# Background steps, store queues and early loads in a one-core step of a hybrid encoder with expert lookup

## The chip, the core and the metric

The kernel runs on one core of a Trainium2 chip. The metric is device microseconds of one execution, the median of several runs. The engines named here are TensorE (PE; its weight loads are PEld), VectorE (DVE), ScalarE (ACT), GpSimd (POOL) and SyncE (SP), which in this kernel only starts transfers. Each engine takes its instructions in order. A transfer that an engine starts sits in that engine's instruction stream, and if it has to wait for something, all that stands behind it on that engine waits too.

## What is computed

One layer of a streaming encoder on 512 prompt tokens and 8 x 16 sample tokens, all in float32:

```python
z = rmsnorm(x, norm_mix_g) @ w_in              # q, k, v, u, vs, gate a, gate b
o = attend(q, k, v, bias, mask, sinks)          # sliding window, a table of relative positions as bias
s = sgu(gelu(u), rmsnorm(gelu(vs)), w_s, b_s)   # chunked spatial gating
x = x + (sigmoid(ga) * (o @ w_pa) + sigmoid(gb) * (s @ w_pb)) @ w_out
xn = rmsnorm(x, norm_ffn_g)
q = xn @ w_query                                # 8 heads, two halves, 128 keys each
# top 16 of the 16 x 16 sums of the two halves' top 16 -> 16 experts per head, g = softmax
y = x + sum over the 128 chosen experts e of g_e * gelu(U[e] . xn) * V[e]
y = rmsnorm(y, norm_final_g)
```

The outputs are y and the new key, value and gating rows. There are 16384 experts with rows of 2048 numbers in U and in V.

## The kernel before

The tokens form five tiles of 128: four prompt tiles (0 to 3) and the sample tile (4, `SAMPLE`). They go in two groups: G1 = (0, 4) first, then G2 = (1, 2, 3). Every projection is a call of `gemm`, which walks over the weight rows in steps of 256: a 512 KB load (`raw`, four buffers) by SP, and for each 128 rows a rounding copy `whi` by ScalarE (L143) and the rest `wlo` by VectorE (L144). TensorE multiplies three times for each tile: x-high with `whi`, x-high with `wlo`, x-low with `whi` (L211 to L213).

The experts are treated in two ways. The tiles of G1 gather: `gather_peer` reads the 128 chosen rows of U, then those of V, one row for each token at a time, 1 MB per gather (L754, by GpSimd), with a product on VectorE for each (L740, L745), and closes with `finish` (norm, scaling L726, store of y L727). The tiles of G2 go dense: `dense_peer` multiplies with all of U in 32 blocks of 512 experts (`U(s)`), weighs the result with a matrix of gates (`wd`, built in `weights` for every token by a matmul of two one-hot products, L789 to L799), and multiplies with all of V in 16 blocks of 1024 experts, each in four column blocks (`V(b, nb)`).

Two queues of generators fill the gaps. `side` holds small work (attention, gating, routing, `weights`, the late steps); `pump`, called after every 256 rows, takes steps from it at a rate of `steps[0]`. `bg` holds the two `gather_peer` generators, tile 0 and then the sample tile; `tick` takes from it at half the GEMM's rate per 256 rows, and these instructions get a low priority. A scheduler orders the instructions of each engine from these priorities, so an order on an engine need not be the order in the code.

The places that the change and the prediction speak of:

- Start. `prep` loads the x tiles transposed (`xT`), scales them and splits them; `start_rows` takes its steps inside the first GEMM (keys and values, `w_kv`) and puts the rest at the front of `side` in its last but one step. `bias_table` looks up the bias rows by a matmul and stores them, repeated 32 times, to `bvd` in device memory (768 KB from 16 partitions). `sample_consts` loads what the sample tile's attention needs: the cached keys and values (`kcT`, `vc`), its new values after a trip through device memory (`vnd`, `vn`), the sinks and the bias.
- Dense stage, first part: U blocks 0 to 11 (`LEAD`) run ahead of any V block. Their activations are stored to device memory (`ad`, L831), since the gates are not ready yet; `late` reads them back. After block 11 the work pools are closed and opened anew with other sizes.
- Dense stage, second part: V blocks 0 to 15, and from block 5 on the U blocks 12 to 31 between them. `RATE_C` is the rate of the background steps in V blocks 0 to 4, `RATE_D` in all later U and V blocks, and `RATE_T` in the last six V column blocks, from where on gathers take their buffers from a larger pool (`deep`, tiles named `m`).
- End: the last V blocks' sums get their squares (L850) and the factor `gfin` (L853), then the row norms scale 12 pieces of 128 x 512, by ScalarE every third (L890) and VectorE the others (L892), and each is stored (L893).

Of the kernel before, what the change touches and what calls it, by code (L numbers as in the profile page):

```python
# [27 lines left out]
RATE_Q = 0.6  # L28
RATE_W = 1.2
RATE_C = 1.3  # L30
RATE_D = 1.63
SQ = 0.6
SW = 1.6
SA = 0.8
# [25 lines left out]
def body(tc, A, O):  # L60
    nc = tc.nc
    with ExitStack() as ctx:
# [22 lines left out]
        def mtile(shape, dt=F32):  # L85
            return mt.tile(shape, dt, name=nm("m"), tag="m")
# [135 lines left out]
        def bias_table():  # L222
            tab = evs((32, 16))
            nc.sync.dma_start(tab, A["table"])
            oh = evs((32, 384))
            nc.sync.dma_start(oh, A["onehot"])
            p = misc()
            nc.tensor.matmul(p[:16, :384], tab, oh, start=True, stop=True)
            bv = evs((16, 384))
            nc.vector.tensor_copy(bv, p[:16, :384])  # L230
            nc.sync.dma_start(bvd, bv.unsqueeze(1).to_broadcast([16, 32, 384]))
            for _ in range(5):
                yield


# [76 lines left out]
        def sample_consts(vnat, out):  # L312
            vnd = dr.tile([128, 128], F32, name="vnd")
            nc.sync.dma_start(vnd, vnat)
            yield
            kc = mtile([128, 2, 8, 128])
            nc.vector.memset(kc, 0.0)
            for kv in range(2):
                nc.sync.dma_start(kc[kv * 64:kv * 64 + 64, kv], A["kcT"][kv * 64:kv * 64 + 64])
            vc = mtile([128, 8, 128])  # L320
            nc.sync.dma_start(vc, A["vc"])
            sk = stat(2)
            nc.sync.dma_start(sk, A["sinks_s"])
            bias = slot((128, 2, 144))
            for kv in range(2):
                nc.sync.dma_start(bias[:, kv, :],
                                  bass.AP(tensor=bvd.tensor, offset=bvd.offset + kv * 8 * 32 * 384 + 127,
                                          ap=[[32 * 384, 8], [383, 16], [1, 144]]))
            vn = mtile([16, 8, 128])
            nc.sync.dma_start(vn, vnd.rearrange("(b t) d -> t b d", b=8))  # L330
            out.extend((kc, vc, vn, sk, bias))
            yield

# [441 lines left out]
        def weights(ti, ijg):  # L775
# [7 lines left out]
            for t0 in range(0, 128, 4):  # L783
# [12 lines left out]
                    nc.tensor.matmul(pw[:, t - t0, :], a, b, start=True, stop=True)  # L796
                w = slot((128, 4, 128))
                nc.scalar.copy(w, pw)  # L798
                nc.sync.dma_start(wd[ti][t0:t0 + 4, :].rearrange("t (i j) -> i t j", i=128), w)  # L799
                yield  # L800

        def dense_peer(G, x2T, r2, x1d):
            n = len(G)
            ad = [[dr.tile([128, 512], F32, name=nm("ad")) for _ in G] for _ in range(LEAD)]
            if True:
# [20 lines left out]
                def U(s, ticks):  # L826
                    def ev(i, ps):
                        a = abuf()
                        nc.scalar.activation(a, ps, AF.Gelu_apprx_tanh, scale=r2[i])
                        if s < LEAD:  # L830
                            nc.sync.dma_start(ad[s][i], a)  # L831
                        else:
                            side.append(h_step(s, i, a))
                    gemm(x2T, 0, KC, A["UT"][s], ev, ticks)
# [50 lines left out]
                for c in range(4):  # L885
                    cs = slice(c * 512, c * 512 + 512)
                    for i, ti in enumerate(G):
                        t = y[i, c]
                        if (c * n + i) % 3 == 0:
                            nc.scalar.activation(t, t, AF.Copy, scale=r[i])  # L890
                        else:
                            nc.vector.tensor_scalar_mul(t, t, r[i])  # L892
                        nc.sync.dma_start(O["y"][ti][:, cs], t)  # L893

        G1, G2 = (0, SAMPLE), (1, 2, 3)
        x1a, r1a, x1b, r1b = [], [], [], []
        start = prep(G1, x1a, r1a, [(i, c) for c in range(4) for i in range(2)])
        next(start)
        next(start)
        side.append(bias_table())  # L900

        def start_rows(kc):
            if kc % 2 == 0 and kc:
                next(start)
                next(start)
            if kc == 6:
                side.insert(0, start)

        nextg = prep(G2, x1b, r1b, [(i, c) for i in range(3) for c in range(4)])

# [103 lines left out]
```

## Time and profile before

| what | us |
|---|---|
| median of 3 runs (lowest, highest) | 3988.98 (3987.25, 3996.61) |
| the profiled execution | 3996.57 |
| its span, first to last instruction | 3994.9 |
| first matmul starts | 7.43 |
| last matmul starts | 3976.26 |
| TensorE busy | 3883.8 |
| VectorE busy | 3153.5 |
| ScalarE busy | 1728.2 |
| GpSimd busy | 829.1 |

The profiled execution is 7.6 us above the median; 1.7 us of it lie outside the span. Busy times are sums over the span; what an engine was idle for, and what ended the wait, is read from the timeline and from the waits. The windows give the same sums for a stretch.

### The profile page before, as it was taken

How to read it: one execution, taken by the hardware profiler on the slowest of the kernel's cores; microseconds unless marked ns; L12 is line 12 of the kernel's file. 1: busy time of each engine (PE TensorE's matmuls, PEld its weight loads, DVE VectorE, ACT ScalarE, POOL GpSimd, SP SyncE). 2: the span in 40 equal slices, each digit the busy share in tenths (PEclk: the TensorE clock that was granted, in tenths of full speed). 3: DMA queues.
4: the chain of work that ended last, by engine and by line, in shares of the span. 5: the costliest groups of instructions: out<-in, count | busy, mean ns of one | idle time of the engine just before them, and what ended most of it. 6: DMA issues, size and time to landing. Idle time of an engine off the chain costs nothing. (4 is left out here: it accounts for less than half of the span.)

```text
span 3994.9 us, 52665 instructions
## 1 busy us (share of the span) xinstructions
PE 3883.8 (97%) x17880; PEld 3177.5 (80%) x17880; DVE 3153.5 (79%) x5421; ACT 1728.2 (43%) x3338; POOL 829.1 (21%) x678
## 2 busy tenths in 40 slices
PE   8999998999999999999999899999999999999998
PEld 6778786877777888877878788877888888888886
DVE  4655769966767987899977688878888888888888
ACT  5665554444444334436665333333333333333333
POOL 1000113211212223211111112222222222222222
PEclk9999999999999999999999999999999999999999
DMA  7666786777878997569988989989998999999987
GB/s 224 204 187 208 248 264 201 273 276 279 311 277 286 336 334 249 206 198 314 327 264 288 338 325 338 342 299 365 338 350 336 353 331 345 345 340 349 346 337 290
DMA packets 333919, 1180.51 MB, mean 296 GB/s; under 512 B 35840, under 2 KB 94784, under 8 KB 267088
## 3 DMA queue, kind: packets, MB, share of 16 engines
q1 hardware_dynamic: 259824, 640.15, 47.9%
q0 software_dynamic: 73824, 536.99, 35.0%
q8 instruction: 141, 2.31, 0.2%
q14 instruction: 130, 1.06, 0.1%
HBM read 1117.69 MB, written 59.31 MB: 295 GB/s over the span
## 5 line engine op out<-in xcount | busy, mean ns | idle before, releaser
L211 PE MATMUL acc<-whi,m 128*128 128x512 f32 (+1 forms) x5232 | 2066.7, 395 | 23.3 <-ACT whi L143 18.3
L212 PE MATMUL acc<-wlo,m 128*128 128x512 f32 (+1 forms) x5232 | 2049.8, 392 | 22.5 <-DVE wlo L144 22.4
L213 PE MATMUL acc<-whi,m 128*128 128x512 f32 (+1 forms) x5232 | 2044.1, 391 | 0.3 <-DVE m L144 0.2
L143 ACT CAST whi<-raw 128x512 fp32r<-128x512 f32 (+1 forms) x1888 | 1157.9, 617 | 1979.3 <-PE acc L213 1646.6
L144 DVE TENSOR_TENSOR wlo<-raw,whi 128x512 fp32r<-128x512 f32 (+1 forms) x1824 | 1221.5, 689 | 526.8 <-ACT whi L143 523.1
L212 PEld LDWEIGHTS acc<-wlo,m 128*128 128x128 f32 x5232 | 990.7, 189 | 227.1 <-DVE wlo L144 34.5
L211 PEld LDWEIGHTS acc<-whi,m 128*128 128x128 f32 x5232 | 989.3, 189 | 225.4 <-ACT whi L143 20.6
L213 PEld LDWEIGHTS acc<-whi,m 128*128 128x128 f32 x5232 | 989.5, 189 | 202.7 <-DVE m L144 0.8
L740 DVE SCALAR_TENSOR_TENSOR gb<-gb,xa 128x2048 f32<-128x2048 f32 x256 | 589.6, 2303 | 79.5 <-DMA gb<-in_U,idx 69.1
L745 DVE SCALAR_TENSOR_TENSOR xa<-gb,hw,xa 128x2048 f32<-128x2048 f32 x239 | 560.3, 2344 | 70.4 <-DMA gb<-in_V,idx 64.1
L754 POOL DMA_INDIRECT gb<-in_V,idx x239 | 318.5, 1333 | 1228.8 <-DVE wlo L144 331.2
L754 POOL DMA_INDIRECT gb<-in_U,idx x256 | 339.6, 1327 | 1018.9 <-ACT whi L143 366.2
L144 POOL TENSOR_TENSOR wlo<-raw,whi 128x512 fp32r<-128x512 f32 x64 | 91.5, 1431 | 261.8 <-ACT whi L143 229.7
L796 PEld LDWEIGHTS pm<-s 128*128 128x128 f32 x768 | 102.6, 193 | 30.5 <-ACT s L793 14.6
L796 PE MATMUL pm<-s 128*128 128x128 f32 x768 | 113.7, 283 | 10.0 <-DVE s L789 8.0
L789 DVE TENSOR_SCALAR s<-io,S 128x128 f32<-128x128 f32 x384 | 114.8, 339 | 3.6 <-DMA wd<-s 3.6
L847 DVE TENSOR_TENSOR s<-s,acc 128x512 f32<-128x512 f32 x180 | 112.5, 678 | 0.0
L144 DVE TENSOR_TENSOR m<-pm,m 128x512 fp32r<-128x512 f32 (+1 forms) x142 | 93.5, 661 | 7.5 <-ACT m L143 6.5
L143 ACT CAST m<-pm 128x512 fp32r<-128x512 f32 (+1 forms) x142 | 79.6, 563 | 16.3 <-PE pm L362 6.3
L798 ACT COPY s<-pm 128x512 f32<-128x512 f32 x96 | 56.5, 588 | 64.8 <-PE pm L796 64.2
L814 DVE TENSOR_TENSOR b<-b,b 128x512 f32<-128x512 f32 x36 | 24.8, 688 | 56.0 <-DMA b<-wd 53.5
L792 ACT ACTIVATE s<-io,S 128x128 f32<-128x128 f32 x192 | 66.7, 398 | 3.6 <-DVE S L782 2.3
(194 smaller groups left out, 1668.7 us busy)
## 6 DMA issues: line engine op xcount, KB each, us to landing
raw<-in_UT SPq DMA_DIRECT2D x256, 512.0 KB, 6.2
raw<-in_VP SPq DMA_DIRECT2D x256, 512.0 KB, 6.5
raw<-in_w_in SPq DMA_DIRECT2D x224, 512.0 KB, 4.6
raw<-in_w_out SPq DMA_DIRECT2D x64, 512.0 KB, 5.4
raw<-in_w_q SPq DMA_DIRECT2D x64, 512.0 KB, 4.5
wd<-s SPq DMA_DIRECT2D x96, 256.0 KB, 6.0
b<-wd SPq DMA_DIRECT2D x96, 256.0 KB, 5.2
raw<-in_w_pa SPq DMA_DIRECT2D x32, 512.0 KB, 4.2
```

The source lines that it names most:

```text
L143: mark[0] = nc.scalar.copy(hi, src).ins
L144: (E or nc.vector).tensor_sub(lo, src, hi.bitcast(F32))
L211: nc.tensor.matmul(o, xh, hi, start=(k == 0), stop=False)
L212: nc.tensor.matmul(o, xh, lo, start=False, stop=False)
L213: nc.tensor.matmul(o, xl, hi, start=False, stop=(k == K - 1))
L740: q = nc.vector.scalar_tensor_tensor(t, t, 1.0, xg, op0=ALU.mult, op1=ALU.mult, accum_out=dots[:, j:j + 1])
L745: q = nc.vector.scalar_tensor_tensor(y, t, hw[:, j:j + 1], y, op0=ALU.mult, op1=ALU.add)
L754: d = nc.gpsimd.indirect_dma_start(out=t, out_offset=None, in_=src, in_offset=bass.IndirectOffsetOnAxis(ap=idx[j // 32][:, j % 32:j % 32 + ...
L789: nc.vector.tensor_scalar(a, io128, tr[:, 0, t:t + 1], tr[:, 2, t:t + 1], op0=ALU.is_equal, op1=ALU.mult)
L792: nc.scalar.activation(b, io128, AF.Abs, bias=tr[:, 3, t:t + 1])
L796: nc.tensor.matmul(pw[:, t - t0, :], a, b, start=True, stop=True)
L847: nc.vector.tensor_add(y[i, nb], x1, ps)
```

## The change

Four groups of edits. `RATE_D` rises from 1.63 to 1.72. The `wd` and `ad` stores are started by ScalarE instead of SP, and so is every third of the last stores of y, the one that ScalarE has scaled itself. `bias_table` is no longer in `side` from the start: it is appended behind `start` near the end of the first GEMM, and it gives up three steps behind its work instead of five. In `sample_consts` the loads of `vn` and the sinks come first, the `kcT`, `vc` and bias loads are divided by two more `yield`s, and the memset of the key tile moves from VectorE to GpSimd.

```diff
@@ -28,7 +28,7 @@
 RATE_Q = 0.6
 RATE_W = 1.2
 RATE_C = 1.3
-RATE_D = 1.63
+RATE_D = 1.72
 SQ = 0.6
 SW = 1.6
 SA = 0.8
@@ -229,7 +229,7 @@
             bv = evs((16, 384))
             nc.vector.tensor_copy(bv, p[:16, :384])
             nc.sync.dma_start(bvd, bv.unsqueeze(1).to_broadcast([16, 32, 384]))
-            for _ in range(5):
+            for _ in range(3):
                 yield
 
 
@@ -313,21 +313,23 @@
             vnd = dr.tile([128, 128], F32, name="vnd")
             nc.sync.dma_start(vnd, vnat)
             yield
+            vn = mtile([16, 8, 128])
+            nc.sync.dma_start(vn, vnd.rearrange("(b t) d -> t b d", b=8))
+            sk = stat(2)
+            nc.sync.dma_start(sk, A["sinks_s"])
             kc = mtile([128, 2, 8, 128])
-            nc.vector.memset(kc, 0.0)
+            nc.gpsimd.memset(kc, 0.0)
             for kv in range(2):
                 nc.sync.dma_start(kc[kv * 64:kv * 64 + 64, kv], A["kcT"][kv * 64:kv * 64 + 64])
+                yield
             vc = mtile([128, 8, 128])
             nc.sync.dma_start(vc, A["vc"])
-            sk = stat(2)
-            nc.sync.dma_start(sk, A["sinks_s"])
+            yield
             bias = slot((128, 2, 144))
             for kv in range(2):
                 nc.sync.dma_start(bias[:, kv, :],
                                   bass.AP(tensor=bvd.tensor, offset=bvd.offset + kv * 8 * 32 * 384 + 127,
                                           ap=[[32 * 384, 8], [383, 16], [1, 144]]))
-            vn = mtile([16, 8, 128])
-            nc.sync.dma_start(vn, vnd.rearrange("(b t) d -> t b d", b=8))
             out.extend((kc, vc, vn, sk, bias))
             yield
 
@@ -796,7 +798,7 @@
                     nc.tensor.matmul(pw[:, t - t0, :], a, b, start=True, stop=True)
                 w = slot((128, 4, 128))
                 nc.scalar.copy(w, pw)
-                nc.sync.dma_start(wd[ti][t0:t0 + 4, :].rearrange("t (i j) -> i t j", i=128), w)
+                nc.scalar.dma_start(wd[ti][t0:t0 + 4, :].rearrange("t (i j) -> i t j", i=128), w)
                 yield
 
         def dense_peer(G, x2T, r2, x1d):
@@ -828,7 +830,7 @@
                         a = abuf()
                         nc.scalar.activation(a, ps, AF.Gelu_apprx_tanh, scale=r2[i])
                         if s < LEAD:
-                            nc.sync.dma_start(ad[s][i], a)
+                            nc.scalar.dma_start(ad[s][i], a)
                         else:
                             side.append(h_step(s, i, a))
                     gemm(x2T, 0, KC, A["UT"][s], ev, ticks)
@@ -890,21 +892,20 @@
                             nc.scalar.activation(t, t, AF.Copy, scale=r[i])
                         else:
                             nc.vector.tensor_scalar_mul(t, t, r[i])
-                        nc.sync.dma_start(O["y"][ti][:, cs], t)
+                        (nc.scalar if (c * n + i) % 3 == 0 else nc.sync).dma_start(O["y"][ti][:, cs], t)
 
         G1, G2 = (0, SAMPLE), (1, 2, 3)
         x1a, r1a, x1b, r1b = [], [], [], []
         start = prep(G1, x1a, r1a, [(i, c) for c in range(4) for i in range(2)])
         next(start)
         next(start)
-        side.append(bias_table())
 
         def start_rows(kc):
             if kc % 2 == 0 and kc:
                 next(start)
                 next(start)
             if kc == 6:
-                side.insert(0, start)
+                side.extend([start, bias_table()])
 
         nextg = prep(G2, x1b, r1b, [(i, c) for i in range(3) for c in range(4)])
```

## Rows read from the trace of the kernel before

**Rows 1.** Part 1 of the page: busy time of each engine, its share of the span and its instructions.

```profile
PE 3883.8 (97%) x17880; PEld 3177.5 (80%) x17880; DVE 3153.5 (79%) x5421; ACT 1728.2 (43%) x3338; POOL 829.1 (21%) x678
```

**Rows 2.** Windows, late dense part: stretch in us and its length; then busy us and instructions of TensorE, its weight loads, VectorE, ScalarE and GpSimd; granted TensorE clock, mean busy share of the DMA engines, GB/s.

```profile
2750.00:3300.00 550.00, 550.00 (x2476) 455.03 (x2475) 466.79 (x584) 191.68 (x314) 144.80 (x108) 1.00 0.92 344
```

**Rows 3.** Windows of the start, columns as in rows 2.

```profile
12.00:16.00 4.00, 4.00 (x23) 4.00 (x22) 2.67 (x6) 1.68 (x5) 0.00 (x0) 1.00 0.86 96
...
16.00:20.00 4.00, 2.05 (x18) 1.84 (x16) 2.33 (x3) 0.34 (x1) 0.00 (x0) 1.00 0.91 102
...
24.00:28.00 4.00, 4.00 (x19) 4.00 (x20) 2.25 (x6) 1.95 (x6) 1.43 (x2) 0.50 1.02 316
```

**Rows 4.** Timeline of the SP queue at the start: start us, duration us, engine, line, operation, out<-in, count (x2 with a long duration spans the time between the two).

```profile
10.88 0.70 SPq L231 DMA_DIRECT2D bvd<-e  x1
...
11.62 4.74 SPq L426 DMA_DIRECT2D S<-in_xT  x2
...
19.95 0.90 SPq L426 DMA_DIRECT2D S<-in_xT  x2
...
41.77 1.18 SPq L319 DMA_DIRECT2D m<-in_kcT  x2
...
43.00 0.58 SPq L321 DMA_DIRECT2D m<-in_vc  x1
...
46.04 11.33 SPq L198 DMA_DIRECT2D raw<-in_w_in  x7
```

**Rows 5.** Timeline of TensorE at the start, two instructions before which it was idle; in brackets the idle us and what ended them.

```profile
23.07 0.58 PE L211 MATMUL acc<-whi,m 128*128 128x256 f32 x1 [5.02 <-ACT m L143]
...
52.40 0.49 PE L211 MATMUL acc<-whi,m 128*128 128x512 f32 x1 [3.59 <-ACT whi L143]
```

**Rows 6.** Timeline of GpSimd at the start: the first operation after its loads of `xT` tiles.

```profile
64.50 0.20 POOL L282 MEMSET S<- 64x128 f32 x1 [35.81 <-DMA S<-bvd]
```

**Rows 7.** Timeline of the SP queue at the border of the U and V blocks.

```profile
2184.76 0.33 SPq L198 DMA_DIRECT2D raw<-in_UT  x1
...
2205.38 1.68 SPq L831 DMA_DIRECT2D ad<-S  x3
...
2207.22 0.34 SPq L198 DMA_DIRECT2D raw<-in_VP  x1
```

**Rows 8.** Timeline at the same border: TensorE's last transposes of old tiles, ScalarE's activation of the last U block, TensorE's first matmul of the V block.

```profile
2193.11 0.60 PE L818 MATMUL pm<-ident,b 128*128 128x128 f32 x4
...
2204.66 2.05 ACT L829 ACTIVATE S<-acc,stats 128x512 f32<-128x512 f32 x3 [8.22 <-PE acc L213]
...
2212.34 0.80 PE L211 MATMUL acc<-whi,m 128*128 128x512 f32 x1 [6.37 <-ACT whi L143]
```

**Rows 9.** The `wd` stores (L799) and `ad` stores (L831) by source line: count, shortest, median and longest issue in ns, first and last start.

```profile
L799 SPq DMA_DIRECT2D wd<-s x96: 359/360/1568, 1809.1 to 2158.8; - x96
...
L831 SPq DMA_DIRECT2D ad<-S x36: 319/332/1321, 1715.0 to 2206.7; - x36
```

**Rows 10.** Window of the stretch with the `wd` stores, columns as in rows 2.

```profile
1809.00:2165.00 356.00, 346.04 (x1859) 289.23 (x1858) 308.92 (x739) 233.12 (x621) 51.03 (x42) 0.99 0.91 302
```

**Rows 11.** The SP queue's own waits, whole span: who waited for what, us in total, times, longest.

```profile
SPq L799 <- ACT s L792: 150.4, 82, 5.1
```

**Rows 12.** Timeline near 2050 us, VectorE and TensorE.

```profile
2049.20 0.69 DVE L814 TENSOR_TENSOR b<-b,b 128x512 f32<-128x512 f32 x1 [8.68 <-DMA b<-wd]
...
2050.89 2.04 PE L796 MATMUL pm<-s 128*128 128x128 f32 x8 [8.03 <-DVE s L789]
```

**Rows 13.** Line 754 by source: the gathers into the deep buffers (`m` tiles): count, shortest, median and longest ns, first and last start.

```profile
L754 POOL DMA_INDIRECT m<-in_V,idx x17: 936/2149/3593, 3876.5 to 3957.2; - x17
```

**Rows 14.** Timeline of VectorE in the tail.

```profile
3967.05 4.73 DVE L745 SCALAR_TENSOR_TENSOR xa<-m,hw,xa 128x2048 f32<-128x2048 f32 x2
...
3977.32 0.68 DVE L853 TENSOR_TENSOR s<-s,b 128x512 f32<-128x512 f32 x1
...
3978.40 2.35 DVE L726 SCALAR_TENSOR_TENSOR xa<-xa,stats,m 128x2048 f32<-128x2048 f32 x1 [0.39 <-DMA m<-in_gfin]
...
3980.67 1.29 DVE L853 TENSOR_TENSOR s<-s,b 128x512 f32<-128x512 f32 x2
...
3982.76 0.49 DVE L892 TENSOR_SCALAR s<-s,stats 128x512 f32<-128x512 f32 x1
```

**Rows 15.** Timeline of the SP queue in the tail.

```profile
3980.78 0.34 SPq L727 DMA_DIRECT2D out_y<-xa  x1
...
3983.36 7.28 SPq L893 DMA_DIRECT2D out_y<-s  x12
```

**Rows 16.** Windows of the tail, columns as in rows 2.

```profile
3985.00:3988.00 3.00, 0.00 (x0) 0.00 (x0) 1.08 (x3) 0.17 (x1) 0.00 (x0) 0.50 1.04 378
...
3990.00:3992.00 2.00, 0.00 (x0) 0.00 (x0) 0.00 (x0) 0.00 (x0) 0.00 (x0) 0.50 1.04 384
...
3992.00:3994.00 2.00, 0.00 (x0) 0.00 (x0) 0.00 (x0) 0.00 (x0) 0.00 (x0) 0.50 0.27 99
```

**Rows 17.** The first finish (tile 0): VectorE's wait, SP's `y` store, and the window of 2660 to 2670 us.

```profile
2662.81 2.35 DVE L726 SCALAR_TENSOR_TENSOR xa<-xa,stats,gb 128x2048 f32<-128x2048 f32 x1 [6.81 <-DMA gb<-in_gfin]
...
2665.19 0.34 SPq L727 DMA_DIRECT2D out_y<-xa  x1
...
2660.00:2670.00 10.00, 10.00 (x46) 8.01 (x45) 7.19 (x10) 6.01 (x9) 1.25 (x1) 1.00 0.69 248
```

## The prediction

> **What bounds the kernel now.** I read the page's busy shares first: TensorE is busy 97% of the span [rows 1]. That is an average, so the next view is the windows of the late dense part: there TensorE is busy all the time, 550.00 of 550 us, with VectorE at 467 us and the DMA engines at a share of 0.92 [rows 2]. Nothing that only unloads another engine can shorten that part. A gain has to come from places where TensorE stands still, so I looked for these in the timeline: the first 55 us, the border between the dense stage's first twelve U blocks and its V blocks (near 2205 us), one hole near 2050 us, and the tail after the last matmul near 3976 us. The diff touches each of the four.
>
> **Start: the bias table is emitted later.** Before, `bias_table` runs in the first GEMM. Its store to `bvd` goes to the SP queue at 10.88 us; the two `xT` loads behind it take SP 4.74 us instead of the 0.9 us of such a pair, and the last pair goes out at 19.95 us [rows 4]. From 12 to 20 us the DMA engines are 0.86 to 0.91 busy and yet move 96 to 102 GB/s [rows 3]: 8 us at about 99 GB/s is 0.79 MB, which is that one store (16 x 32 x 384 x 4 bytes = 0.79 MB). TensorE waits 5.02 us at 23.07 us for the `xT` chunk that was behind it [rows 5], and from 24 to 28 us it runs at a granted clock of 0.50, which costs another 2 us [rows 3]. The change emits the table after the remaining `start` steps, so the store leaves this place: minus 5.0 us, with up to 2 us of clock on top. The store still has to run. Pump steps are counted alike (2 left of `start`, 1+5 of the table and 2 of `sample_consts` become 2, 1+3 and 4), so attention starts at the same step, and the store now falls into the first Q block, some 38 to 50 us. There TensorE has a second hole, 3.59 us at 52.40 us [rows 5]: `kcT` and `vc`, 1 MB in all, went out before the next weight load, at 46.04 us [rows 4]. Spread over three steps they no longer do; the 8 us of the store come instead. I set these two against each other. The bounds: 0 (the whole hole comes back at the new place) to 5.0+2.0+3.6 = 10.6 us gained. I take 5. The `kc` memset goes from VectorE to GpSimd, which stands idle 35.81 us there [rows 6]; at 0.20 us for 128 columns of half the partitions, 2048 columns are at most 16 x 0.20 = 3.2 us, hidden in that idle time; without it, `sample_consts` would be that much later.
>
> **Border of U and V: activation stores by ScalarE.** SP issues one raw load at 2184.76 us and then stands at the first `ad` store until 2205.38 us, since the store waits for ScalarE's gelu of the last U block; the first load for V, queued behind it, goes out at 2207.22 us [rows 7]. TensorE is then idle 6.37 us until 2212.34 us [rows 8]. On ScalarE's queue the same store waits where its producer is, and SP is free. The V loads reuse the space of the old tiles, whose last reader among the `b` tiles is the transpose at 2193.11 us [rows 8], so a load could be out some 13 us earlier than 2207.22 us, enough for the hole to vanish. Against this, the order in which ScalarE takes the new casts and the gelu is not known: if the gelu stays first, its three pieces end near 2206.7 us [rows 8] and only a cast and a subtraction are left, a hole of some 2 us. So minus 2 to minus 6.4 us if SP is freed, 0 if the loads don't move; I take minus 4.
>
> **Gate stores by ScalarE.** 96 `wd` stores cost SP 0.36 us each and 36 `ad` stores 0.33 us (longest 1.57 and 1.32 us) [rows 9]. ScalarE has issued no DMA in this run, so its price is bounded by nothing below and 1.57 us above; I take SP's, 96 x 0.36 = 35 us between 1809 and 2165 us, where ScalarE has 356 - 233 = 123 us idle [rows 10]. That idle time hides them; without it each issue delays the next cast by its own length. VectorE is 309 of 356 us busy there and waits for those casts, so some leaks out: plus 1 us (0 to 8). SP stops waiting for these copies, 150.4 us in 82 waits [rows 11], but TensorE loses only 10 us in this stretch [rows 10], and 8.03 of them are one chain, VectorE waiting 8.68 us for a load of gates just stored [rows 12]. An earlier store could shorten it: 0 to minus 8, taken as 0.
>
> **More background steps.** Each loop step of a GEMM adds half the rate; a U block has 8, a V block 4. At 1.72 instead of 1.63 the 20 late U blocks give 20 x 4 x 0.09 = 7.2 more steps and the 38 V blocks up to block 14 give 38 x 2 x 0.09 = 6.8: 14 steps, one gather each. Before, 17 gathers are left for the deep buffers, the last at 3957.2 us [rows 13]; after, 3. A late matmul takes 550/2476 = 0.22 us [rows 2], so a V block of 72 takes 16 us; at three steps in each, the sample tile's finish is then emitted in the last V block but four, some 64 us earlier. The stretch with the new rate (20 x 144 + 38 x 72 matmuls) lasts about 1250 us. There the 14 gathers cost VectorE 14 x 2.37 = 33 us [rows 14] and the DMA engines 14 x 1.05 MB / 1250 us = 12 GB/s on 344: the share goes from 0.92 to about 0.95. Both have that room [rows 2], so 0, and 0 to 4 us if a load is late.
>
> **Tail.** Before, VectorE does the last two gathers' products, then at 3978.40 us the sample tile's scaling (2.35 us) between the prompt tiles' own steps, so that the first output scaling starts at 3982.76 us [rows 14]. Without it the two L853 steps follow at once and end near 3979.2 instead of 3981.96 us: all later steps come 2.8 us earlier. The stores: 12 of 256 KB leave SP in 7.28 us behind the sample tile's 1 MB [rows 15], and the DMA engines are full (1.04 at 378 GB/s) from 3985 to past 3992 us [rows 16]. Now 3.15 MB remain, 8.2 us at 384 GB/s: from 3980.6 plus 0.9 to start they end near 3989.7 instead of 3992.5 us. Minus 2.8 us (1.5 to 4). Four stores moved to ScalarE save up to 4 x 0.6 = 2.4 us of issue, but the transfers bound this stretch, so at most 0.8 us of the 2.8 is theirs.
>
> The Trainium skill (DMA: Bandwidth & Descriptors, "Issuing engines are not separate DMA queues") says the same against this edit: whichever engine starts a transfer, it shares the same 16 DMA engines, and only issue time is saved. The share of 1.04 agrees; by the rule alone the split is worth nothing.
>
> The earlier finish has a price of its own. At the first one VectorE waited 6.81 us for the `gfin` load and SP stood at the `y` store until 2665.19 us with raw loads behind it, but TensorE stayed at 10.00 of 10 us [rows 17]. Plus 1 us (0 to 7).
>
> **Sum.** -5 -4 +1 -2.8 +1 = -9.8 us. The profiled execution took 3996.57 us (span 3994.9 and 1.7 around it), 7.6 us above the median of 3988.98. It would come to about 3987, and the median to about 3979.
>
> **Rivals.** (1) Holes close altogether: 8 to 10 us at the start, 6.4 at the border with its clock, some of the 8.03 us hole, the tail: minus 13 to minus 24, about 3971. For it: three of these holes hang on SP standing at one store. Against: at the start DMA time is only moved. (2) Holes move and don't close: the bias store stops the first Q block as it stopped the first GEMM, and V's loads still wait for the old tiles. Only the tail is left: about 3987. For it: the DMA share near 50 us is as high as before it. (3) Slower: ScalarE's issue time decides. It is on the way to every cast, and it has 123 us of room for 96 stores: up to 1.28 us each is hidden. At SP's longest, 1.57 us, the stretch grows by 96 x 1.57 - 123 = 28 us, less the gains: about 4007; it passes plus 12 us from 1.6 us per issue on. Against: the median is 0.36 us. That the late dense part gets shorter by the rate itself is excluded by the busy time there [rows 2].
>
> **Chances.** About 0.3%, 12 us, is what a measurement of this kernel can tell from no change. The forecast has 0.42, with its own range of 3973 to 3986; 0.06 of that is beyond 12 us. Rival 1 has 0.34, rival 2 0.13, rival 3 0.11. So faster 0.06+0.34 = 0.40, same 0.36+0.13 = 0.49, slower 0.11. The range goes from 3966, which leaves out the far end of rival 1, to 3993, which takes in rival 2 and leaves out rival 3.
>
> **What would show it.** Right: no TensorE wait near 18 to 23 us and the `bvd` store near 40 us or later; the first V load before 2200 us and a TensorE hole under 3 us there; about 3 gathers into `m` tiles, the last gather near 3890 us; the first output scaling some 3.5 us after the last matmul instead of 6. Wrong: a new wait of ScalarE or its casts behind its own stores between 1809 and 2165 us; a hole of 5 us or more in the first Q block; TensorE waiting for casts in the last five V blocks, where the finish now is; or a DMA share near 1.0 with late raw loads after 2575 us.

## The result: slower, by 33 us

The changed kernel takes 4022.52 us (median of 4 runs, 4019.35 to 4025.95), the kernel before 3988.56 us beside it. The ratio is 1.0082 (95% interval 1.0069 to 1.0095): slower, where 3979 us was forecast, in a range from 3966 to 3993 us. The profiled execution took 4019.35 us, its span is 4017.7 us. Below, a difference in us is the ratio of a run less 1, times the median of the kernel before that was measured beside it.

The first view is the windows of the dense stage's first part: the stretch in which the gates are built, and the 100 us around the border of U and V. Columns: stretch, its length, then busy us (and instructions) of TensorE, of its weight loads, of VectorE, ScalarE and GpSimd; the granted clock; the DMA share; GB/s.

```profile
1800.00:2140.00 340.00, 330.06 (x1748) 278.27 (x1747) 288.15 (x655) 219.54 (x552) 48.84 (x41) 0.99 0.91 303
2140.00:2240.00 100.00, 74.94 (x373) 61.45 (x372) 59.65 (x124) 46.44 (x109) 13.51 (x8) 0.85 0.66 226
```

The same two stretches before:

```profile
1800.00:2140.00 340.00, 325.57 (x1740) 271.92 (x1741) 300.67 (x715) 224.38 (x594) 48.83 (x40) 0.98 0.91 303
2140.00:2240.00 100.00, 93.64 (x440) 77.09 (x440) 67.59 (x98) 40.99 (x81) 14.82 (x11) 0.97 0.86 301
```

TensorE is idle 9.9 us in the first stretch and 25.1 us in the second; before, it was 14.4 and 6.4 us, and the whole border had one hole of 6.37 us [rows 8]. So the loss is not where the gates are built but behind it. The timeline of TensorE there, with the idle time before an instruction and what ended it in brackets:

```profile
2193.07 0.66 PE L820 MATMUL pm<-ident,b 128*128 128x128 f32 x4 [0.33 <-DVE m L144]
2206.61 1.09 PE L820 MATMUL pm<-ident,b 128*128 128x128 f32 x4 [12.88 <-DVE b L816]
...
2212.65 1.09 PE L820 MATMUL pm<-ident,b 128*128 128x128 f32 x4 [3.59 <-DVE b L816]
2217.63 1.09 PE L820 MATMUL pm<-ident,b 128*128 128x128 f32 x4 [3.89 <-DVE b L816]
2219.91 1.65 PE L211 MATMUL acc<-whi,m 128*128 128x512 f32 x3 [1.19 <-ACT whi L143]
2223.86 0.80 PE L212 MATMUL acc<-wlo,m 128*128 128x512 f32 x1 [2.30 <-DVE wlo L144]
```

TensorE waits for the late steps: transposes of the gated activations (L820 is the L818 of before), which wait for VectorE's product (L816), which waits for a load of gates. The hole costs more than its idle time: four transposes that took 0.66 us ahead of it take 1.09 us behind it, and the mean granted clock of the 100 us is 0.85, against 0.97 before. Why that load is late stands in the waits of SP's queue from 2140 to 2240 us (total, times, longest), in SP's timeline, and in the row of the gate stores (issue time min/median/max in ns, first and last start):

```profile
SPq L99 <- DMA wd<-s: 40.3, 3, 25.7
```

```profile
2199.75 0.33 SPq L99 DMA_DIRECT2D b<-wd  x1
...
2209.45 0.43 SPq L198 DMA_DIRECT2D raw<-in_VP  x1
```

```profile
L801 ACTq DMA_DIRECT2D wd<-s x96: 366/366/406, 1800.2 to 2193.4; - x96
```

The last gate store now starts at 2193.4 us; before, the last one started at 2158.8 us. SP stands up to 25.7 us at the load of gates just stored, and the first V load, queued behind it, leaves at 2209.45 us, later than the 2207.22 us of before [rows 7]. The 96 starts took ScalarE 366 ns each (median); SP's took 360 ns [rows 9].

Why are the gates 35 us later, if TensorE waits hardly longer while they are built? The view for this is the groups of TensorE between the first and the last gate matmul (L798 here, L796 before), first of the changed kernel, then of the same kernel with gate stores on SP and the rate at 1.63 (e8 below):

```profile
L213 PE MATMUL acc<-whi,m 128*128 128x512 f32 x421 | 172.0, 409 | 0.0
L211 PE MATMUL acc<-whi,m 128*128 128x512 f32 x420 | 170.7, 408 | 0.0
L212 PE MATMUL acc<-wlo,m 128*128 128x512 f32 x420 | 170.7, 406 | 0.8 <-DVE wlo L144 0.8
L798 PE MATMUL pm<-s 128*128 128x128 f32 x768 | 119.8, 278 | 9.7 <-ACT s L795 3.9 <-DVE s L791 3.2 <-DVE s L797 2.2
```

```profile
L211 PE MATMUL acc<-whi,m 128*128 128x512 f32 x355 | 144.7, 407 | 0.0
L212 PE MATMUL acc<-wlo,m 128*128 128x512 f32 x354 | 142.2, 402 | 0.0
L213 PE MATMUL acc<-whi,m 128*128 128x512 f32 x355 | 141.2, 398 | 0.0
L798 PE MATMUL pm<-s 128*128 128x128 f32 x768 | 112.3, 281 | 4.0 <-DVE s L791 2.4 <-ACT s L795 1.4
```

The same 768 records of gate matmuls have 1261 GEMM matmuls between them instead of 1064. That is not a matter of waiting: TensorE takes its instructions in the order in which the scheduler wrote them before the run, and with the stores on ScalarE the scheduler wrote another order. Read from the compiled order, the counts are 1062 and 1260; the traces of all runs whose compiled count is given below agree to within 3. At 0.22 us a matmul the 198 more are 44 us. The U blocks run ahead of the gates, and at the border, where both must be done, the rest of the gates and of the late steps is waited for.

The other places. The start went as forecast. The timelines of SP and of TensorE, and the window that had the low clock:

```profile
12.95 0.33 SPq L428 DMA_DIRECT2D S<-in_xT  x1
...
39.83 0.69 SPq L231 DMA_DIRECT2D bvd<-e  x1
```

```profile
29.14 1.18 PE L211 MATMUL acc<-whi,m 128*128 128x512 f32 x2 [4.32 <-ACT whi L143]
...
52.03 0.49 PE L211 MATMUL acc<-whi,m 128*128 128x512 f32 x1 [2.84 <-ACT whi L143]
```

```profile
24.00:28.00 4.00, 0.83 (x7) 0.62 (x6) 0.00 (x0) 1.73 (x3) 0.00 (x0) 1.00 0.96 335
```

The last xT load leaves at 12.95 instead of 19.95 us [rows 4], the wait of 5.02 us at 23.07 us [rows 5] is gone, and one of 4.32 us comes 6 us later. The granted clock from 24 to 28 us is 1.00 instead of 0.50 [rows 3], though TensorE is busy there for 0.83 us only. The table store leaves at 39.83 us, and the hole at 52 us is 2.84 instead of 3.59 us. The tail: TensorE's last matmul, VectorE's timeline, and the row of the gathers into deep buffers on GpSimd:

```profile
4001.19 0.39 PE L213 MATMUL acc<-whi,m 128*128 128x512 f32 x1
```

```profile
4002.22 1.89 DVE L855 TENSOR_TENSOR s<-s,b 128x512 f32<-128x512 f32 x3
...
4004.92 0.49 DVE L894 TENSOR_SCALAR s<-s,stats 128x512 f32<-128x512 f32 x1
```

```profile
L756 POOL DMA_INDIRECT m<-in_V,idx x3: 936/938/1010, 3901.3 to 3920.4; - x3
```

Three gathers are left for the deep buffers instead of 17 [rows 13], the sample tile's scaling has left the tail, and the first output scaling starts 3.7 us after the last matmul's start, against 6.5 us before [rows 14].

The late dense part lost too. Its two halves as windows, then ScalarE's waits for weights in the first:

```profile
2690.00:3320.00 630.00, 612.94 (x2727) 501.30 (x2726) 538.00 (x666) 209.59 (x349) 162.48 (x130) 1.00 0.93 350
3320.00:3900.00 580.00, 579.43 (x2602) 479.05 (x2601) 504.56 (x497) 200.31 (x327) 163.26 (x120) 1.00 0.94 355
```

```profile
ACT whi L143 <- DMA raw<-in_VP: 59.9, 22, 4.8
ACT whi L143 <- DMA raw<-in_UT: 28.4, 10, 5.3
```

The first half before:

```profile
2690.00:3320.00 630.00, 625.20 (x2799) 515.83 (x2798) 536.65 (x670) 216.69 (x355) 164.95 (x125) 1.00 0.93 348
```

TensorE is idle 17.1 us from 2690 to 3320 us; before, it was 4.8 us, and the middle was busy all the time [rows 2]. The casts wait 88 us for raw loads, against 32 us before, and the DMA share of 0.93 shows nothing of it: it was 0.93 before too. A raw load there takes a median of 7.4 us from its start to its landing, against 7.0 us before, while VectorE, which frees the buffers of these loads, is busy 538 us, against 537 us. So the loads themselves take longer; that VectorE also frees some buffers later was not tested apart.

### The profile page after: what moved, and what is told of

Read it like the earlier page. It is cut to its first block, busy times and chain, and to the rows that moved or that the text cites. A ratio compares the mean times of both kernels' runs of the same rounds, so it can differ in the third digit from the quotient of the medians.

```text
span 4017.7 us, 52539 instructions
## 1 busy us (share of the span) xinstructions
PE 3886.3 (97%) x17880; PEld 3177.2 (79%) x17880; DVE 3152.7 (78%) x5420; ACT 1733.1 (43%) x3338; POOL 801.6 (20%) x679
## 5 line engine op out<-in xcount | busy, mean ns | idle before, releaser
L143 ACT CAST whi<-raw 128x512 fp32r<-128x512 f32 (+1 forms) x1888 | 1152.7, 617 | 1923.9 <-PE acc L213 1508.8
L144 DVE TENSOR_TENSOR wlo<-raw,whi 128x512 fp32r<-128x512 f32 (+1 forms) x1824 | 1225.0, 693 | 489.4 <-ACT whi L143 484.4
L747 DVE SCALAR_TENSOR_TENSOR xa<-gb,hw,xa 128x2048 f32<-128x2048 f32 x253 | 594.0, 2348 | 69.7 <-DMA gb<-in_V,idx 69.5
L756 POOL DMA_INDIRECT gb<-in_V,idx x253 | 335.9, 1327 | 1264.1 <-DVE wlo L144 309.3
L756 POOL DMA_INDIRECT gb<-in_U,idx x256 | 323.5, 1264 | 1010.4 <-ACT whi L143 343.7
L144 POOL TENSOR_TENSOR wlo<-raw,whi 128x512 fp32r<-128x512 f32 x64 | 90.9, 1421 | 260.3 <-ACT whi L143 229.6
L798 PEld LDWEIGHTS pm<-s 128*128 128x128 f32 x768 | 114.8, 192 | 31.1 <-ACT s L795 10.5
L798 PE MATMUL pm<-s 128*128 128x128 f32 x768 | 119.8, 278 | 9.7 <-ACT s L795 3.9
L144 DVE TENSOR_TENSOR m<-pm,m 128x512 fp32r<-128x512 f32 (+1 forms) x142 | 93.8, 664 | 18.4 <-ACT m L143 17.7
L143 ACT CAST m<-pm 128x512 fp32r<-128x512 f32 (+1 forms) x142 | 79.6, 563 | 40.6 <-PE pm L820 29.2
L820 PE MATMUL pm<-ident,b 128*128 128x128 f32 x384 | 59.9, 280 | 27.1 <-DVE b L816 26.8
L816 DVE TENSOR_TENSOR b<-b,b 128x512 f32<-128x512 f32 x36 | 24.9, 692 | 74.3 <-DMA b<-wd 71.4
```

Source lines behind the costliest of these rows:

```text
L143: mark[0] = nc.scalar.copy(hi, src).ins
L144: (E or nc.vector).tensor_sub(lo, src, hi.bitcast(F32))
L747: q = nc.vector.scalar_tensor_tensor(y, t, hw[:, j:j + 1], y, op0=ALU.mult, op1=ALU.add)
L756: d = nc.gpsimd.indirect_dma_start(out=t, out_offset=None, in_=src, in_offset=bass.IndirectOffsetOnAxis(ap=idx[j // 32][:, j % 32:j % 32 + ...
L820: nc.tensor.transpose(pt[:, j, :], w[:, j * 128:j * 128 + 128], ident)
```

## The experiments

**Which edit loses (e1 to e4).** e1 is the changed kernel with its gate stores back on SP (the first pair of lines), e2 the one with the rate back at 1.63 (the second pair). e3 is the kernel before with the first pair the other way round, the gate stores alone, and e4 with the second, the rate alone.

```diff
-                nc.scalar.dma_start(wd[ti][t0:t0 + 4, :].rearrange("t (i j) -> i t j", i=128), w)
+                nc.sync.dma_start(wd[ti][t0:t0 + 4, :].rearrange("t (i j) -> i t j", i=128), w)
...
-RATE_D = 1.72
+RATE_D = 1.63
```

> The changed kernel with the wd stores back on SP, all else as changed. Theory G (the wd stores on ScalarE make each gate step longer, the gates fall 35 us behind and the last U block ends before them, so the border of U and V loses about 26 us): about 20 us come back, some 4000 us, last wd store before the last U block's gelu, no TensorE wait of 12.9 us near 2206 us. Theory R (the higher rate is the cause, by late weight loads after the tile switch near 2690 us): no change, 4020.

> The changed kernel with RATE_D back at 1.63. Theory R: the 13 to 17 us that are lost between 2690 and 3200 us come back, less the 3 us of the tail, some 4007 us, no casts waiting for raw loads past 2800 us. Theory G: the border's loss stays, and if it is all, the time stays at 4020.

> The kernel before with only the wd stores moved to ScalarE. Theory G: slower by some 20 us, about 4009, with the hole at the border and gate steps of 4.0 us instead of 3.7. Theory R: 3989, no change.

> The kernel before with only RATE_D at 1.72. Theory R: slower by some 10 us, about 3999 (loss of 13 in the dense part, 3 back in the tail). Theory G: faster by the tail's 3 us, about 3986.

| run | median us | ratio to before (interval) | difference us |
|---|---|---|---|
| e1, gate stores on SP | 3996.48 | 1.0015 (1.0005 to 1.0025) | +6 |
| e2, rate 1.63 | 4015.65 | 1.0065 (1.0048 to 1.0081) | +26 |
| e3, gate stores alone | 4006.49 | 1.0046 (1.0029 to 1.0063) | +18 |
| e4, rate alone | 3996.74 | 1.0015 (1.0004 to 1.0026) | +6 |

Both edits lose. The gate stores cost 18 us alone and 27 us out of the changed kernel (the result less e1); the rate costs 6 us alone and 7 us out of the changed kernel (the result less e2).

**What the others are worth (e5 to e8).** On top of the kernel before, all edits of the start alone (e5; its core is the first diff), the activation stores alone (e6, the second) and the split of the y stores alone (e7, the third). e8 is the changed kernel with both pairs of lines above, gate stores and rate, undone.

```diff
-        side.append(bias_table())
...
-                side.insert(0, start)
+                side.extend([start, bias_table()])
```

```diff
-                            nc.sync.dma_start(ad[s][i], a)
+                            nc.scalar.dma_start(ad[s][i], a)
```

```diff
-                        nc.sync.dma_start(O["y"][ti][:, cs], t)
+                        (nc.scalar if (c * n + i) % 3 == 0 else nc.sync).dma_start(O["y"][ti][:, cs], t)
```

> The kernel before with the changes of the start alone: the bias table after the remaining start steps, the sample tile's cache loads spread over three steps, the kc memset on GpSimd. Theory S (the forecast's term): the 5 us wait near 23 us is gone and nothing after it gives the time back: 5 to 10 us less, about 3982. Rival: the time that is won at the start is given back later, because the dense stage is paced by transfers and not by when it begins: the first evictions 5 to 8 us earlier, but the end within 2 us of before, 3988 to 3990.

> The kernel before with the 36 activation stores alone issued by ScalarE. Theory A (the forecast's term): SP is free at the border of U and V, its first load for V leaves before 2200 us, and the TensorE hole of 6.37 us shrinks to 2 us or less: 4 us less, about 3985. Rival 1: the loads for V wait for the old tiles in any case, the hole stays at 5 to 7 us: no change, 3989. Rival 2: the issue time on ScalarE delays the gate steps as that of the gate stores did, 36 stores against 96: plus 5 to 7 us, about 3995.

> The kernel before with the split of the y stores alone (every third by ScalarE). Theory T (the forecast's term): the transfers bound the tail, so at most 0.8 us is won: 3988 to 3989. Rival: the issue on one queue bounds it, 4 stores of 0.6 us less: 3986.5.

> The kernel after with both losing edits undone: gate stores on SP again and the late rate at 1.63, so that the start, the activation stores and the y split remain. Theory 1 (the two edits cost what their own runs showed and the others win what the forecast gave them): 5 of the start and 4 of the border less, about 3980. Theory 2 (the losses add: 26 us for the gate stores and 7 for the rate, off 4022.5): 3989.5, so that the other parts are worth nothing together. Theory 3: the activation stores lose on ScalarE too: 3992 to 3998.

| run | median us | ratio to before (interval) | difference us |
|---|---|---|---|
| e5, start | 3980.01 | 0.9986 (0.9977 to 0.9994) | -6 |
| e6, activation stores | 3986.66 | 1.0001 (0.9991 to 1.0010) | 0 |
| e7, y stores | 3988.54 | 1.0003 (0.9994 to 1.0011) | +1 |
| e8, both undone | 3981.23 | 0.9986 (0.9977 to 0.9994) | -6 |

The start's term holds; its parts (the table, the spread loads, the memset) were not measured apart. The activation stores alone do what was forecast at the border, as TensorE's timeline of e6 shows, with SP's first V load above it:

```profile
2182.29 0.33 SPq L198 DMA_DIRECT2D raw<-in_VP  x1
...
2196.98 0.49 PE L211 MATMUL acc<-whi,m 128*128 128x512 f32 x1 [2.44 <-ACT whi L143]
```

The hole shrinks from 6.37 to 2.44 us, but the median does not show the 4 us; its interval goes from -3.6 to +4.0 us. Part of the reason is in the trace: over the whole 100 us from 2140 to 2240 us TensorE is idle 4.9 us in e6, against 6.4 us before, since other waits come back beside the smaller hole. The y split is worth nothing: in e7, SP takes as long for 8 stores as it took for 12 [rows 15].

```profile
3976.30 7.23 SPq L893 DMA_DIRECT2D out_y<-s  x8
```

This is what the Trainium skill says (DMA: Bandwidth & Descriptors, "Issuing engines are not separate DMA queues"): stores started by two engines share the same 16 DMA engines. e8 falls on e5: what is left of the change is the start. e8 also prices the rate a third time, since e1 is e8 with the rate at 1.72: +6 against -6, 12 us, about twice what the rate costs alone.

**Order, issue time or queue (e9 to e12).** Three explanations of the gate stores' cost were set against each other: the scheduler's order (O), ScalarE's time per gate step on the chip (I), and stores that land late through ScalarE's queue (Q). `ACT_OH` is the number of one-hot products of each gate step (four tokens) that ScalarE builds, two instructions each; VectorE builds the others. `SW` is the rate of the side steps in U blocks 0 to 11. e9 and e10, the first two diffs (the second cut to its first and last lines; those between are only indented), are the changed kernel at rate 1.63 (e2) with the edit; e11 and e12 are e8 with the edit.

```diff
-ACT_OH = 2
+ACT_OH = 1
```

```diff
+                with tc.high_priority(offset=100):
-                pw = misc((128, 4, 128))
+                    pw = misc((128, 4, 128))
...
-                nc.scalar.dma_start(wd[ti][t0:t0 + 4, :].rearrange("t (i j) -> i t j", i=128), w)
+                    nc.scalar.dma_start(wd[ti][t0:t0 + 4, :].rearrange("t (i j) -> i t j", i=128), w)
```

```diff
-ACT_OH = 2
+ACT_OH = 3
```

```diff
-SW = 1.6
+SW = 1.4
```

> The kernel after with the rate back at 1.63 and, in each gate step, one of the two one-hot pairs of ScalarE given to VectorE (two ScalarE instructions of 0.31 to 0.40 us less in a step, the store's start of 0.37 us stays on ScalarE). The order of the instructions on TensorE, which is fixed before the run, now puts 1062 GEMM matmuls between the first and the last gate matmul, as with SP's stores, instead of 1260. Theory O (the order decides): the end is that of the kernel with SP's stores, about 3981, and the hole at the border is 2 us. Theory I (ScalarE's time in a step decides on the chip): 0.7 us less and 0.37 more, so about 3981 too. Theory Q (stores through ScalarE's queue land too late for the loads behind them): no change to 4012 to 4016.

> The kernel after with the rate back at 1.63, and the gate steps given a higher priority in the scheduler; the instructions and their engines are the same, only the order changes: 1121 GEMM matmuls between the first and the last gate matmul instead of 1260 (1062 with SP's stores). Theory O: the loss of 31 us shrinks with the order, (1121-1062)/(1260-1062) of 31 is 9 us, so about 3990. Theory I: the same starts on the same engine cost the same, about 4012. Theory Q: 4012 to 4016 too.

> Gate stores on SP, rate 1.63, and one more one-hot pair of each gate step on ScalarE (two instructions of 0.31 to 0.40 us more, 0.7 us a step, twice what a store's start takes there). The order stays: 1072 GEMM matmuls between the first and the last gate matmul. Theory O: 3981 to 3984. Theory I: 96 steps of 0.7 us more on ScalarE lag more than 96 starts of 0.37 us did: 4012 or more.

> Gate stores on SP, rate 1.63, and the pace of the side steps in the stage lowered from 1.6 to 1.4, so that the order itself is stretched with no start on ScalarE: 1203 GEMM matmuls between the first and the last gate matmul. Theory O: (1203-1062)/(1260-1062) of 31 is 22 us more, about 4003, with SP held at the border by the loads of the last gates. Theory I and theory Q: no cost of a start, 3981.

The windows from 2140 to 2240 us, for e8, e9, e11 and e12 in turn, and for e10 with the stretch before it:

```profile
2140.00:2240.00 100.00, 97.61 (x443) 79.86 (x443) 70.69 (x80) 36.43 (x62) 14.98 (x13) 0.98 0.92 335
```

```profile
2140.00:2240.00 100.00, 97.27 (x444) 79.64 (x443) 70.67 (x83) 36.86 (x63) 14.04 (x13) 0.98 0.93 332
```

```profile
2140.00:2240.00 100.00, 97.68 (x455) 79.84 (x454) 73.09 (x99) 43.52 (x88) 12.95 (x12) 0.98 0.90 321
```

```profile
2140.00:2240.00 100.00, 85.05 (x421) 70.16 (x420) 67.27 (x143) 49.87 (x120) 10.33 (x8) 0.90 0.76 253
```

```profile
1800.00:2140.00 340.00, 323.91 (x1714) 271.60 (x1714) 288.81 (x678) 221.37 (x565) 45.58 (x41) 0.97 0.89 297
2140.00:2240.00 100.00, 91.34 (x445) 75.54 (x444) 69.67 (x122) 47.13 (x103) 14.66 (x11) 0.97 0.85 287
```

| run | gate stores by | GEMM matmuls between the gates | TensorE idle 2140 to 2240 us | median us | ratio (interval) | difference us |
|---|---|---|---|---|---|---|
| e9 | ScalarE, one pair less there | 1062 | 2.7 | 3981.92 | 0.9985 (0.9975 to 0.9995) | -6 |
| e10 | ScalarE, gates with priority | 1121 | 8.7 | 4001.53 | 1.0038 (1.0027 to 1.0050) | +15 |
| e11 | SP, one pair more on ScalarE | 1072 | 2.3 | 3988.22 | 1.0006 (0.9997 to 1.0016) | +2 |
| e12 | SP, side steps slower | 1203 | 15.0 | 3998.68 | 1.0024 (1.0014 to 1.0035) | +10 |

e9 has all 96 stores on ScalarE and loses nothing against e8: Q falls. It does not tell O from I, as its expectation says: the pair that ScalarE no longer builds is worth about as much of its time as the starts (ScalarE is busy 37 us less than in e8 from 1800 to 2140 us, and 96 starts take 35 us). e11 has twice the starts' time as additional work on ScalarE, and costs 8 us against e8: ScalarE's time costs something, but 67 us of it only 8. By that measure the 35 us of starts are worth some 4 us; that is an estimate, since e11 also takes some 28 us of work off VectorE. e12 has no start on ScalarE, only a stretched order, and shows the hole: 15.0 us, and 15 us against e8 where the order foretold 22. And e10, with the same instructions on the same engines as e2 and only another order, is 11 us faster than e2. So O stands for most of the loss. It does not work as a straight line. In e12 the gates also begin later (first gate matmul at 1818.6 us instead of 1798.5 in e8), and its last gate store, at 2196.9 us, is as late as that of the changed kernel, with a hole 10 us smaller. And e10, for which 9 us were expected, lost 21 against e8. With priority the waiting moved from the border into the gate stretch, where TensorE is idle 16.1 us, as TensorE's waits in e10 from 1809 to 2140 us show (L799 is the L798 of the others):

```profile
PE pm L799 <- ACT s L796: 8.4, 5, 5.3
PE pm L799 <- DVE s L792: 6.9, 3, 5.6
```

These are waits for the one-hot products of ScalarE and of VectorE, so the time of these engines counts where the gates are packed more closely. How much of e10's loss it is was not measured.

**Which half pays for the higher rate (e13, e14).** As many more background steps, all in V blocks 10 and later (e13) or all before (e14). Both are e8 with the edit; e14 has the two values exchanged.

```diff
 RATE_D = 1.63
+RATE_E = 1.81
...
-                            U(s, RATE_D)
+                            U(s, RATE_D if b < 10 else RATE_E)
...
-                        V(b, nb, RATE_T if deep[0] else RATE_C if b < LEAD // 2 - 1 else RATE_D)
+                        V(b, nb, RATE_T if deep[0] else RATE_C if b < LEAD // 2 - 1 else RATE_D if b < 10 else RATE_E)
```

> The kernel with gate stores on SP, rate 1.63 up to V block 9, and 1.81 from block 10 on: as many more background steps as 1.72 gives, all in the second half. Theory D (the loss of the higher rate lies in the first half, from 2690 to 3320 us, where its gathers make the raw loads late; the second half has room): TensorE idle 3 to 4 us from 2690 to 3320 us and under 5 us from 3320 to 3900 us, and the end 3 us before that of the rate 1.63, for the shorter tail: about 3979. Rival (any such gather costs the same, wherever it stands): the second half loses 8 to 12 us: about 3990.

> The same with 1.81 up to V block 9 and 1.63 from block 10 on. Theory D: TensorE idle 13 us or more from 2690 to 3320 us, the end 8 us or more behind the rate 1.63: 3990 or more. Rival (any such gather costs the same): as e13, about 3990 for both. If neither half loses, the loss of the rate 1.72 comes from somewhere else, and both are at 3979.

e13 took 3996.47 us, 1.0018 (1.0007 to 1.0029), e14 3995.76 us, 1.0025 (1.0015 to 1.0036), both more than the 3990 us of the rival. First the two halves in e8:

```profile
2690.00:3320.00 630.00, 626.61 (x2811) 517.44 (x2811) 530.44 (x652) 217.70 (x358) 166.88 (x124) 1.00 0.91 344
3320.00:3900.00 580.00, 578.80 (x2600) 477.85 (x2599) 497.21 (x502) 200.25 (x329) 162.14 (x115) 1.00 0.92 345
```

The two halves in e13 and then in e14, each followed by ScalarE's waits for V's raw loads in the half that has the steps (L144 is the L143 of the others):

```profile
2690.00:3320.00 630.00, 627.02 (x2813) 517.97 (x2812) 534.22 (x662) 216.75 (x356) 165.97 (x126) 1.00 0.92 346
3320.00:3900.00 580.00, 568.46 (x2526) 466.52 (x2525) 506.37 (x495) 196.74 (x322) 176.83 (x123) 0.99 0.94 358
```

```profile
ACT whi L144 <- DMA raw<-in_VP: 50.5, 19, 5.6
```

```profile
2690.00:3320.00 630.00, 612.32 (x2707) 501.10 (x2706) 541.40 (x654) 207.59 (x344) 173.03 (x133) 0.99 0.93 353
3320.00:3900.00 580.00, 578.24 (x2597) 477.88 (x2596) 488.59 (x492) 201.87 (x329) 162.00 (x113) 1.00 0.92 343
```

```profile
ACT whi L144 <- DMA raw<-in_VP: 72.4, 26, 6.5
```

The idle time goes where the steps go: 3.4 and 1.2 us in e8, 3.0 and 11.5 us in e13, 17.7 and 1.8 us in e14. ScalarE's waits for V's raw loads, 21.9 and 28.1 us in e8 in the same stretches, grow to 50.5 and 72.4 us. The rival is right: no half has room, and theory D falls. Both lose 13 to 16 us against e8, the shorter tail included, as e1 with its 12 us does.

**Where the 27 us come from (e15, e16).** e15 is e5 and e16 is e6 with the gate stores by ScalarE: together with the start alone, and together with the activation stores alone, both at rate 1.63.

```diff
-                nc.sync.dma_start(wd[ti][t0:t0 + 4, :].rearrange("t (i j) -> i t j", i=128), w)
+                nc.scalar.dma_start(wd[ti][t0:t0 + 4, :].rearrange("t (i j) -> i t j", i=128), w)
```

> The kernel before with the changes of the start and the gate stores by ScalarE; activation stores on SP, rate 1.63. The order puts 1231 GEMM matmuls between the first and the last gate matmul, as with the gate stores alone. Theory O: the hole at the border is that of the gate stores alone, 16 us of TensorE idle time from 2140 to 2240 us, and the start's 6 us are kept: 12 us more than before, about 4000. Rival (what the start gains is lost at the border, since the late gates set its end): 18 us more, 4006.

> The kernel before with the gate and the activation stores by ScalarE; start as before, rate 1.63. The order: 1260. Theory O: the activation stores on ScalarE stretch the order on from 1231, TensorE idle 24 us from 2140 to 2240 us, 8 us more than with the gate stores alone: 26 us more than before, about 4014. Rival (the activation stores cost nothing here either, as alone): 18 us more, 4006.

e15 took 3998.51 us, 1.0036 (1.0022 to 1.0049), 14 us more than before; 12 and 18 us both lie in its interval, so it tells little. e16 took 4022.36 us, 1.0088 (1.0073 to 1.0104): 35 us more (29 to 41), twice the gate stores alone and more than the 26 us that theory O gave. The border of e3, e15 and e16 in turn:

```profile
2140.00:2240.00 100.00, 83.74 (x409) 69.18 (x409) 67.00 (x125) 47.48 (x107) 12.60 (x10) 0.88 0.74 257
```

```profile
2140.00:2240.00 100.00, 82.51 (x400) 67.36 (x399) 66.09 (x123) 45.44 (x102) 11.77 (x10) 0.90 0.75 269
```

```profile
2140.00:2240.00 100.00, 73.19 (x372) 60.80 (x372) 57.94 (x131) 47.21 (x113) 8.71 (x7) 0.85 0.61 194
```

With 1231 matmuls in the order TensorE is idle 16.3 and 17.5 us there, with 1260 it is 26.8 us. The activation stores, worth nothing alone, stretch the order on when the gate stores are on ScalarE too, and cost 17 us more (12 us by e2 against e15, where the start and the y split are in). The parts add up within their intervals: -6 for the start, 18 for the gate stores, 12 to 17 for the activation stores on top, 6 to 7 for the rate, in sum 30 to 36; measured were 33.

## Why the prediction was wrong

- **Start, -5:** right. Measured alone -6 (-9 to -2). The table store fell where it was said to, and no hole of 5 us came in the first Q block. The memset on GpSimd took 1.81 us, within its bound.
- **Border, -4:** right in its mechanism for the activation stores alone (hole 6.37 to 2.44 us, with the first V load 25 us earlier); the time did not show it. In the changed kernel the sign turned: with the gate stores on ScalarE too, the gates were not done, SP stood at them instead of at the activation store, and the activation stores cost 12 to 17 us. Two terms that were priced apart were not independent, since one order holds both.
- **Gate stores, +1 (0 to 8):** this is the step that failed; measured were 18 us alone and 27 us out of the changed kernel. Each start took 0.366 us, as taken, and ScalarE's room hides most of that: estimated from e11, it is some 4 us. But the step priced instructions inside an unchanged order. The section on the kernel says that a scheduler orders the instructions of each engine; that it might write another order for the same code with the stores on another engine was not asked. It did, and the gates' last store came 35 us later, though TensorE waited hardly longer than before until the border (10.5 against 10.0 us between the first and the last gate matmul). Rival 3 had the sign, with another mechanism: it needed 1.6 us per issue for 12 us, and 0.366 us came with the loss.
- **More background steps, 0 (0 to 4):** wrong in size. A load was late, as the bound's condition said, but not once: e13 and e14 show 10 and 15 us more TensorE idle time than e8 (4.6 us in both halves) for 14 steps, and the rate costs 6 us alone and 12 us on top of e8, after the tail has given some back. That the DMA engines "have that room" was read from a share of 0.92, an average that hardly moved (0.91 and 0.92 in the halves of e8, 0.93 and 0.94 where e14 and e13 put the steps).
- **Tail, -2.8:** right. From the last matmul's start to the end it takes 16.5 us instead of 18.6, and the first output scaling comes 3.7 us after the last matmul (3.5 forecast). It is the rate's: e4, without the y split, has the same 3.7 us and takes 15.6 us, while every run at rate 1.63 takes between 17 and 22 us. The y split's share of it is nothing.
- **Earlier finish, +1:** no run separates it; it is part of the rate's loss.
- **The hole at 2050 us** [rows 12], taken as a chance of up to 8 us, is no property of the edit. e4 differs from the kernel before only in a rate that is used later, and TensorE's idle time from 1800 to 2140 us is 14.4 us before and 5.3 us there; e1, e8, e13 and e14, which also differ only in that rate, have 7.6, 4.0, 9.8 and 6.1 us. So the hole was most likely that of one execution, and may be why the profiled one lay 7.6 us above the median.

The version that beats both kernels is e8 or e9: 3981 to 3982 us, 0.14% below the kernel before and 1% below the changed one; e5 shows that the start alone brings it.

What stays open: which cost in the scheduler makes it move the gates when ScalarE has the starts beside two one-hot pairs in a step, but not when it has only one pair with the starts (e9) or three pairs without them (e11); why the priority of e10 trades part of the border's hole for waits in the gate stretch; and how much of the loss is ScalarE's time.

## What to carry to other kernels

Where a scheduler writes each engine's order, price a moved instruction only after looking at the order it yields: count the main loop's matmuls between the first and the last instruction of the moved work, before any run. Here the work that fell behind cost next to nothing where it was done; the 15 to 27 us of idle TensorE came at the next point where both streams had to meet. And in a stretch where TensorE is busy all the time and weights come just in time, do not take an average DMA share below 1 for room: here, at 0.92 and 0.93, a gather more cost about 1 us in either half.

## What the runs showed of the hardware beside this

Single executions of one kernel differ by more than most terms of the sum: e8's 11 runs lie between 3972.97 and 3987.22 us, and its profiled one is the fastest of them. A profile shows where the time goes; whether a term of 4 us is there, only many runs can tell, and for the activation stores even 12 could not.

A start of a 256 KB store cost ScalarE 366 ns and SP 360 ns (medians of the 96 gate stores), and the stores landed 5.5 us after their start from ScalarE and 6.0 us from SP (medians of the changed kernel and of the kernel before). By these medians a store that ScalarE starts is not slower; between e9 and e8 they are 5.6 and 5.9 us.
